# Down's seven-product pairs, GpSimd's transfers in up, and re-laid weights in an encoder block on one core

## The chip, the core and the metric

The kernel runs on one core of a Trainium2 chip. The metric is the device time of one execution in microseconds. Three runs of the kernel before gave 1123.14, 1123.25 and 1123.6 us, a median of 1123.25 us. The profile was taken on an execution of its own.

## The reference

One layer of an encoder: 256 tokens, model width 2048, feed-forward width 5632, all in float32. Every sub-layer is wrapped in RMS norms. `@` is a matrix product.

```python
hn = rmsnorm(h, mix_norm_pre)
z, xbc, dt_raw, u = split(hn @ w_in)
mix = concat(ssd_mixer(z, xbc, dt_raw), pool_mixer(u)) @ w_out
h = h + rmsnorm(mix, mix_norm_post)
hn = rmsnorm(h, ffn_norm_pre)
gate, val = split(hn @ w_up)                  # 2048 -> 2 x 5632
gate = dwconv_centred(gate, conv_w, conv_b)   # 3 taps along the tokens
ff = (gelu(gate) * val) @ w_down              # 5632 -> 2048
h = h + rmsnorm(ff, ffn_norm_post)
gate = sigmoid(rmsnorm(h, ple_norm_pre) @ w_ple_gate)
h = h + rmsnorm(gate * (p @ w_ple), ple_norm_post)
```

## The kernel before

**Products.** A float32 operand is kept as two parts, hi (rounded by ScalarE to the format that TensorE multiplies, L152) and lo (the rest, a subtraction on VectorE, L153). A product then takes three matmuls: hi by hi, hi by lo, lo by hi. `split` (L141) makes the two parts of a piece of weights; there are five buffers for hi parts and five for lo parts, and three for raw pieces as they come from memory (`raw`, L156). A raw piece is 128 partitions by 2048 values, 1 MB. All weights come through the DMA queue of one engine, SyncE (SP), in program order of the issues; a load waits there until its buffer is free.

**Stages in time.** dtu, xbc and z are the parts of the input projection, with the mixer's own work between their matmuls. wo is the output projection, ple0 the first half of the small projection of p. Then come up (11 groups `s`, each a gate block `ga` and a value block `va`), down (`dn`), ple1, the gate product (`gt`) and the tail. The stages stand behind one another on TensorE.

**Up.** `feature_pairs` (L340) computes 256 features: two raw pieces, each split in two halves of 1024 columns. There are 88 such raw pieces, here called slots. After each, `aside()` (L196) takes the next entry of the list `work` and runs its jobs: this is where work for later stages is laid aside. Behind the gate block stand the convolution (VectorE, L428), gelu (ScalarE, L884) and a multiplication by the row norm `rfb` on GpSimd (L885); behind the value block the product `hid` (VectorE, L895).

**Down.** `token_major` (L291) takes the hidden features in 22 pairs of 128, for each of two halves of the output columns. An ordinary pair (256 hidden features, 256 tokens, 1024 columns) takes 2 x 2 x 2 x 3 = 24 matmuls of 512 columns. A pair in `dn_fast` is a fast one: `seven_products` (L239) treats it as 2 x 2 blocks and needs seven block products in place of eight, 21 matmuls. For that it needs four sums of blocks on the hidden side (`hid_sums`, L920: four 128-wide VectorE operations, a ScalarE copy, a 512-wide VectorE operation) and four on the weights' side. `combine` (L269) adds the products up. Before, 12 of the 22 pairs of each half are fast; the hidden sums of four pairs (`dn_keep`) are kept in memory from the first half for the second.

**The weights' sums.** They are made during up. `block_sums` (L208) has a job `fetch` (load the piece of w_down into a page), two slots later `add` (`add_blocks`, L232: one 1024-wide and two 512-wide additions on VectorE), one slot later `store` (write the sums to DRAM). There are 28 blocks, 24 for down and 4 for the gate product, one every three slots; the last two are held in pages. In down a fast pair loads from DRAM the three raw blocks that it needs and the page of sums. All of these loads and stores go through SP's queue, among the weights, each behind the one before it (`load`, L116). There are 13 pages of 1 MB.

**Between down and gate.** `back` (L937), before pair 13 of the second half, loads h again, which was stored before up. `first_gate` (L943), before pair 16, loads the first piece of w_ple_gate and makes its parts apart from the splits: ScalarE writes the negated hi part, GpSimd issues a transfer that adds the weights to it, ScalarE writes hi. The dictionary `at` (L955) says where they stand.

**Order.** A scheduler puts the instructions of each engine in order when the kernel is built; every engine then works in that order. `tc.issue_after(x)` keeps an instruction behind x. Names in the profile: `ug_1l` is the lo part of a gate piece in up, `dnb` a block of w_down fetched for its sums, `dns` the stored sums, `hs` the parts of a hidden pair, `he`/`hd`/`hsum` its sums, `gtf` the first gate piece, `hb` h loaded again.

Of the kernel before, what the change touches and what calls it, by code (L numbers as in the profile page):

```python
# [11 lines left out]
F32 = mybir.dt.float32  # L12
# [4 lines left out]
P = 128  # L17
# [34 lines left out]
def build(nc, a, out):  # L52
    x = a["x"][0]
    w_in, w_out, w_up = a["w_in"][0], a["w_out"][0], a["w_ffn_up"][0]
    w_down, w_gate, w_ple = a["w_ffn_down"][0], a["w_ple_gate"][0], a["w_ple"][0]
    out = out[0]

    with tile.TileContext(nc) as tc, \
# [37 lines left out]
        c_dt = DSSD + 1536  # L96
        r0 = wp.tile([P, 2048], F32, tag="raw", bufs=3, name="dtur0")
        for n in range(2):
            first = ins(nc.scalar.dma_start(r0[:, n * 352:(n + 1) * 352],
                                            w_in[:P, c_dt + n * 352:c_dt + (n + 1) * 352]))  # L100
# [15 lines left out]
        def load(dst, src, ahead=False):  # L116

            with tc.issue_after(last["dma"]) if last and not ahead else nullcontext():
                return ins(nc.sync.dma_start(dst, src))

# [35 lines left out]
        def raw(name, src, a_, b_):  # L156
            r = wp.tile([P, 2048], F32, tag="raw", bufs=3, name=name)
            if src is None:
                return r
            last["dma"] = load(r[:, :a_ * b_].rearrange("p (a b) -> p a b", a=a_), src, True)  # L160
            return r
# [34 lines left out]
        def aside():  # L196

            for job in (work.pop(0) if work else ()):
                job()
# [32 lines left out]
        def add_blocks(r):  # L232

            v = r.rearrange("p (b c) -> p b c", b=4)
            nc.vector.tensor_add(v[:, 0:2], v[:, 0:2], v[:, 1::2])  # L235
            nc.vector.tensor_add(v[:, 3], v[:, 3], v[:, 0])
            nc.vector.tensor_add(v[:, 2], v[:, 2], v[:, 3])

        def seven_products(name, stage, w, k0, c0, a_, acc, alt, start, stop):  # L239
# [3 lines left out]
            if (stage, c0, k0) in sums_:  # L243
                r = raw(f"{name}r", None, 0, 0)
# [6 lines left out]
                b11 = split(f"{name}a", r[:, :512], 512)  # L251
                b2 = split(f"{name}b", r[:, 512:1536], 1024)
            else:
                r = t = raw(f"{name}r", w[k0 * P:(k0 + 2) * P, c0:c0 + 1024]
                            .rearrange("(k p) c -> p k c", p=P), 2, 1024)
                b11 = split(f"{name}a", r[:, :512], 512)
                b2 = split(f"{name}b", r[:, 1024:], 1024)
                add_blocks(r)
            t13 = split(f"{name}c", t[:, :1024], 1024)
            t42 = split(f"{name}d", t[:, 1024:], 1024)  # L260
            for x, (wh, wl), c, o, own in (
                    ("a11", b11, 0, alt[0], True), ("a12", b2, 0, acc[0][0], False), ("s4", b2, 512, acc[0][1], False),
                    ("s1", t13, 0, alt[1], True), ("s3", t13, 512, alt[2], True), ("a22", t42, 0, acc[1][0], False),
                    ("s2", t42, 512, alt[3], True)):
# [26 lines left out]
        def token_major(name, w, c0, ks, get, acc, tail=1, fast=(), alt=None, sums=None, at=()):  # L291
# [3 lines left out]
            for u in range(nu):  # L295
# [3 lines left out]
                if u in fast:  # L299
                    if u == fast[0]:  # L300
# [3 lines left out]
                r = None if f"{name}{k0}_0" in ready else raw(f"{name}r{k0}", w[k0 * P:(k0 + 2) * P, c0:c0 + 1024]  # L304
                                                               .rearrange("(k p) c -> p k c", p=P), 2, 1024)
# [8 lines left out]
                for t, (o, c), (k, wh, wl), q in order:  # L314
                    xh, xl = (v[:, t * P:(t + 1) * P] for v in get(k))
                    xx, ww = ((xh, wh), (xh, wl), (xl, wh))[q]
                    mm(o, xx, ww[:, c:c + o.shape[-1]], k == ks[0] and q == 0, k == ks[-1] and q == 2)
# [3 lines left out]
                aside()  # L321

        def feature_major(name, w, c0, get, acc):

            for u in range(4):
                r = raw(f"{name}r{u}", w[u * 512:(u + 1) * 512, c0:c0 + 512]
                        .rearrange("(k p) c -> p k c", p=P), 4, 512)
# [12 lines left out]
        def feature_pairs(name, w, c0, get, acc):  # L340


            for u in range(2):
                r = raw(f"{name}r{u}", w[u * 1024:(u + 1) * 1024, c0:c0 + 256]
                        .rearrange("(k p) c -> p k c", p=P), 8, 256)
# [8 lines left out]
                aside()  # L354
# [88 lines left out]
        for u in range(0, NK, 2):  # L443
            r = [wp.tile([P, 2048], F32, tag="raw", bufs=3, name=f"dtur{u}") if u else r0, page(f"dtur{u + 1}")]
            for j in range(2):
                k = u + j
                if k == 0:
                    last["dma"] = load(r[0][:, 704:1056], w_in[:P, c_dt + 704:c_dt + 1056])
# [3 lines left out]
                for c0, c1 in ((0, 704), (704, 1056)) if k == 1 else ((0, 1056),):  # L452
                    last["dma"] = load(r[j][:, c0:c1], w_in[k * P:(k + 1) * P, c_dt + c0:c_dt + c1])
# [29 lines left out]
        with tc.issue_after(half[0]), tc.issue_after(half[1]):  # L483
# [11 lines left out]
            for a_ in range(4):  # L495
# [17 lines left out]
        load(pmat.rearrange("p (g s t) -> p g s t", g=4, s=2),  # L513
             a["pool_matrix"].rearrange("g (s p) t -> p g s t", p=P))
        poolw = page("poolw")
        load(poolw.rearrange("p (g c d) -> p g c d", g=4, c=2),
             a["pool_w"][0].rearrange("g (c p) d -> p g c d", p=P))
# [122 lines left out]
        def xbc(slab):  # L640
            acc = main(f"xbc{slab}")
            feature_major(f"xb{slab}", w_in, DSSD + slab * 512, hn, acc)
# [29 lines left out]
        def skip(t):  # L672
            nc.gpsimd.tensor_tensor(by_head(y[:, t * 1024:(t + 1) * 1024]), by_head(xs[:, t * 1024:(t + 1) * 1024]),
                                    dsk.unsqueeze(2).to_broadcast([P, H, 64]), op=ALU.mult)

        def mix(t, g):
# [8 lines left out]
            nc.gpsimd.tensor_add(y[:, c0:c0 + 512], y[:, c0:c0 + 512], tm)  # L685
# [45 lines left out]
        token_major("z", w_in, 0, list(range(NK)), hn, zacc)  # L731
# [42 lines left out]
        def pair_sums(name, s, o, a11, a21, a12, a22):  # L774

            s1, s2, s3, s4 = (s[:, i * P:(i + 1) * P] for i in range(4))
# [5 lines left out]
            nc.vector.tensor_sub(o[:, 512:], s[:, :512], o[:, :512].bitcast(F32))  # L782
            return {f"s{i + 1}": (o[:, i * P:(i + 1) * P], o[:, 512 + i * P:512 + (i + 1) * P]) for i in range(4)}
# [81 lines left out]
        dn_fast, gt_fast, dn_keep = ((2, 3, 5, 7, 8, 10, 12, 13, 15, 16, 18, 19), (2, 3, 5, 7, 8, 10, 12, 13, 15, 16, 18, 19)), ((4, 6), (1, 2)), (3, 8, 13, 18)  # L865
# [4 lines left out]
        for i, w_ in enumerate(which[2:] + which[:2]):  # L870
            for j, jobs in enumerate(block_sums(*w_, i >= len(which) - 2)):
                work[3 * i + 2 + j].extend(jobs)
        hid = []
        for s in range(DFF // 512):
            sc = mid(f"gr{s}")
            for i in range(2):
                ga = main(f"ga{s}{i}")
                feature_pairs(f"ug{s}{i}", w_up, s * 512 + i * 256, hf, ga)
# [6 lines left out]
            nc.gpsimd.tensor_tensor(cv.rearrange("p (f t) -> p f t", f=4), cv.rearrange("p (f t) -> p f t", f=4),  # L885
                                    rfb.unsqueeze(1).to_broadcast([P, 4, L]), op=ALU.mult)
            for i in range(2):
                va = main(f"va{s}{i}")
                feature_pairs(f"uv{s}{i}", w_up, DFF + s * 512 + i * 256, hf, va)
# [9 lines left out]
        def get_hid(k):  # L899
            if k % 2 == 0:  # L900
                t = lp.tile([P, 1024], F32R, tag="hs", bufs=2, name=f"hs{k}")
                src = hid[k // 8][:, (k % 8) * L:(k % 8 + 2) * L]
                nc.scalar.copy(t[:, :512], src)  # L903
                nc.vector.tensor_sub(t[:, 512:], src, t[:, :512].bitcast(F32))  # L904
# [13 lines left out]
        keep, kept = [], {}  # L918

        def hid_sums(k):  # L920


            (h1, l1), (h2, l2) = get_hid(k), get_hid(k + 1)
            if k not in kept:
                src = hid[k // 8][:, (k % 8) * L:(k % 8 + 2) * L]
                n = dn_keep.index(k // 2) if k // 2 in dn_keep else -1
                if n >= 0 and n % 2 == 0:
                    keep.append(page(f"hsum{k}", F32R))
                o = keep[-1][:, n % 2 * 1024:(n % 2 + 1) * 1024] if n >= 0 else mid(f"he{k}", F32R)
                d = pair_sums(f"hd{k}", mid(f"hd{k}"), o, *(src[:, i * P:(i + 1) * P] for i in range(4)))  # L930
                if n >= 0:
                    kept[k] = d
            else:
                d = kept[k]
# [8 lines left out]
        def first_gate():  # L943

            r, hi, lo = page("gtf"), page("gtfh", F32R), page("gtfl", F32R)
            src = w_gate[:2 * P, :1024].rearrange("(k p) c -> p k c", p=P)
            last["dma"] = load(r.rearrange("p (k c) -> p k c", k=2), src)
            nc.scalar.activation(lo, r, AF.Copy, scale=-1.0)
            nc.gpsimd.dma_start(lo.rearrange("p (k c) -> p k c", k=2), src, accum_op=ALU.add)
            nc.scalar.copy(hi, r)  # L950
            for j in range(2):
# [3 lines left out]
                      fast=dn_fast, sums=hid_sums, at={13: back, 16: first_gate})  # L955
# [105 lines left out]
def constants():  # L1061
    return {"pool_matrix": pool_matrix()}
# [16 lines left out]
```

## Time and profile before

| | |
|---|---|
| median of three runs | 1123.25 us (1123.14 to 1123.6) |
| the profiled execution | 1123.11 us; its span 1121.3 us, 1.8 us around it |
| granted TensorE clock | 0.997 |
| transferred | 300.87 MB, mean 268 GB/s, 145996 packets, 98560 of them under 2 KB |
| GpSimd's own transfers | 272 packets, 1.05 MB (one transfer, `gtfl`) |

Stages on TensorE, by the chain of work in order of time: dtu to 52.6 us, xbc to 142.4, z to 198.7, wo to 287.1, ple0 and the start of up to 319.9, up to 789.0, down to 1016.7, ple1 and gate to about 1101, the tail to 1121.3.

How to read it: times are microseconds from the start of the span unless marked ns. PE is TensorE, PEld its weight loads, DVE VectorE, ACT ScalarE, POOL GpSimd, SP SyncE; "SPq" is an engine's queue of instructions that are not counted as busy. A row names the line of the kernel, the engine, the operation, output <- inputs, and how often. "[2.79 <-DMA x]" behind a row is idle time of that engine before the instruction, and what ended it. In a row of groups the number after the bar is the busy time, the next the mean of one in ns, and then the idle time before the group. "to landing" is from the issue of a transfer to its end. Busy times of pipelined neighbours overlap, so the pitch from start to start is a little under the duration shown.

### The profile page before, as it was taken

The numbers are of one execution on the slowest core, as the hardware profiler recorded it, in microseconds if no ns is written. First come the engines' busy times: TensorE is split into PE (matmuls) and PEld (weight loads), VectorE is DVE, ScalarE is ACT, GpSimd is POOL, SyncE is SP. The second block draws the span as 40 slices with busy tenths as digits, with TensorE's granted clock in tenths as the row PEclk, the third lists the DMA queues.
The fourth block names the chain that finished last, engine by engine and source line by source line (L and its number), as shares of the span: only waits on it lengthen the run. The fifth ranks groups of instructions, "written<-read, shape, count | busy, mean of one in ns | idle before, by whom it ended". The sixth has DMA issues, their size and how long they took to land.

```text
span 1121.3 us, 15775 instructions
## 1 busy us (share of the span) xinstructions
PE 1109.1 (99%) x5971; PEld 956.4 (85%) x5971; DVE 925.2 (83%) x1275; ACT 663.9 (59%) x927; POOL 76.2 (7%) x86
## 2 busy tenths in 40 slices
PE   9999999999999999999999999999999999999996
PEld 9999987888888888888888888888888888888875
DVE  6569895799898877877877768888899999889795
ACT  6847663555764554554545445445677777786672
POOL 0200004200110100000000000000000000001001
PEclk9999999999999999999999999999999999999998
DMA  9862447456789989989999898996969688995663
GB/s 363 310 207 96 170 161 269 151 188 190 252 308 347 328 300 336 314 289 309 333 330 314 276 330 289 325 304 224 339 185 334 221 286 301 383 318 177 230 235 109
DMA packets 145996, 300.87 MB, mean 268 GB/s; under 512 B 5504, under 2 KB 98560, under 8 KB 137856
## 3 DMA queue, kind: packets, MB, share of 16 engines
q1 hardware_dynamic: 145360, 298.45, 78.6%
q0 software_dynamic: 272, 1.05, 0.5%
q8 instruction: 47, 0.77, 0.3%
q10 hardware_dynamic: 288, 0.36, 0.1%
q14 instruction: 29, 0.24, 0.1%
HBM read 268.38 MB, written 31.46 MB: 267 GB/s over the span
## 4 chain that ended last, share of the span: by engine, by line
PE 96%; ACT 1%; DVE 1%; issue 1%; POOL 1%; POOLq 0%; DVEq 0%; ACTq 0%
PE va L87 22%; PE ga L87 21%; PE dna L87 14%; PE woa L87 7%; PE xbc L87 6%; PE gt L87 5%; PE dtu L87 4%; PE z L87 4%; PE dns L87 3%; PE dn0s L87 1%; PE dn1s L87 1%; PE ple L87 1%; PE pw L87 1%; PE yd L87 0%; PE gts L87 0%
## 5 line engine op out<-in xcount | busy, mean ns | idle before, releaser
L87 PE MATMUL ga<-wox,ug_0h 128*128 128x512 f32 x352 | 125.5, 395 | 0.0
L87 PE MATMUL ga<-wox,ug_1h 128*128 128x512 f32 x352 | 125.1, 394 | 0.0
L87 PE MATMUL va<-wox,uv_1h 128*128 128x512 f32 x352 | 124.8, 393 | 0.0
L87 PE MATMUL va<-wox,uv_0h 128*128 128x512 f32 x352 | 124.8, 393 | 0.0
L87 PE MATMUL ga<-wox,ug_1l 128*128 128x256 f32 x352 | 99.1, 282 | 0.0
L87 PE MATMUL ga<-wox,ug_0l 128*128 128x256 f32 x352 | 99.1, 282 | 0.0
L87 PE MATMUL va<-wox,uv_1l 128*128 128x256 f32 x352 | 99.1, 281 | 0.0
L87 PE MATMUL va<-wox,uv_0l 128*128 128x256 f32 x352 | 99.1, 281 | 0.0
L87 PEld LDWEIGHTS va<-wox,uv_1h 128*128 128x128 f32 x352 | 66.1, 188 | 15.0
L87 PEld LDWEIGHTS va<-wox,uv_0h 128*128 128x128 f32 x352 | 66.1, 188 | 15.0
L87 PEld LDWEIGHTS ga<-wox,ug_0h 128*128 128x128 f32 x352 | 66.1, 188 | 14.9
L87 PEld LDWEIGHTS ga<-wox,ug_1h 128*128 128x128 f32 x352 | 66.1, 188 | 14.9
L87 PEld LDWEIGHTS ga<-wox,ug_0l 128*128 128x128 f32 x352 | 66.2, 188 | 0.1
L87 PEld LDWEIGHTS ga<-wox,ug_1l 128*128 128x128 f32 x352 | 66.2, 188 | 0.0
L87 PEld LDWEIGHTS va<-wox,uv_0l 128*128 128x128 f32 x352 | 66.2, 188 | 0.0
L87 PEld LDWEIGHTS va<-wox,uv_1l 128*128 128x128 f32 x352 | 66.2, 188 | 0.0
L885 POOL TENSOR_TENSOR fc<-fc,rfb 128x1024 f32<-128x1024 f32 x11 | 28.0, 2547 | 438.6 <-ACT fc L884 438.6
L87 PE MATMUL dna<-dn_0h,hs 128*128 128x512 f32 x160 | 50.1, 393 | 0.0
L87 PE MATMUL dna<-dn_1h,hs 128*128 128x512 f32 x160 | 49.9, 393 | 0.0
L235 DVE TENSOR_TENSOR dnb<-dnb 128x1024 f32<-128x1024 f32 x24 | 30.8, 1283 | 17.8 <-DMA dnb<-w_ffn_down 17.6
L903 ACT CAST hs<-hid 128x512 fp32r<-128x512 f32 x44 | 27.2, 617 | 23.2 <-PE dna L87 14.8
L904 DVE TENSOR_TENSOR hs<-hid,hs 128x512 fp32r<-128x512 f32 x44 | 30.2, 686 | 9.8 <-ACT hs L903 9.7
(1903 smaller groups left out, 3105.3 us busy)
## 6 DMA issues: line engine op xcount, KB each, us to landing
dnb<-w_ffn_down SPq DMA_DIRECT2D x24, 1024.0 KB, 10.4
dns<-dnb SPq DMA_DIRECT2D x22, 1024.0 KB, 7.4
dn0r<-w_ffn_down SPq DMA_DIRECT2D x10, 1024.0 KB, 6.0
dn1r<-w_ffn_down SPq DMA_DIRECT2D x10, 1024.0 KB, 7.1
zr<-w_in SPq DMA_DIRECT2D x8, 1024.0 KB, 5.1
dtur<-w_in SPq DMA_DIRECT2D x14, 528.0 KB, 8.7
wo0r<-w_out SPq DMA_DIRECT2D x7, 1024.0 KB, 5.6
wo1r<-w_out SPq DMA_DIRECT2D x6, 1024.0 KB, 5.5
```

Of the source, the lines that this page charges most:

```text
L87: last["pe"] = ins(nc.tensor.matmul(o, lhsT, rhs, start=start, stop=stop, skip_group_check=True))
L235: nc.vector.tensor_add(v[:, 0:2], v[:, 0:2], v[:, 1::2])
L885: nc.gpsimd.tensor_tensor(cv.rearrange("p (f t) -> p f t", f=4), cv.rearrange("p (f t) -> p f t", f=4), rfb.unsqueeze(1).to_broadcast([P, ...
L903: nc.scalar.copy(t[:, :512], src)
L904: nc.vector.tensor_sub(t[:, 512:], src, t[:, :512].bitcast(F32))
```

## The change

1. All weights are laid out anew on the host, in contiguous pieces of 128 x 2048 values as the kernel loads them, so that each partition's row is 8 KB (up had 1 KB rows, down 4 KB). In the pieces for pairs the blocks stand as B12, B11, B21, B22, so a fast pair loads its three raw blocks with one transfer of 6 KB rows.
2. Fast pairs in down: 14 of 22 per half, before 12. The hidden sums of eight pairs (`dn_stored`) are made during up by jobs of their own, stored to DRAM and loaded again in both halves of down; `dn_keep` is gone. The order of the seven products changes.
3. 32 block sums (28 for down, 4 for gate), fetched at slot 5*i//2 + 5, added three slots later, stored one slot after that. The addition is four 512-wide operations, each on the result of the one before.
4. The fetches, the stores, and the stores and loads of the hidden sums are issued by GpSimd (`load_aside`), in program order. Ahead of each slot's jobs GpSimd copies one column of the lo part of that slot's second half (`pace`), so the jobs' transfers go out when VectorE has written that part.
5. The multiplication by `rfb` in up, `skip` and the addition of `ym` in z move from GpSimd to VectorE.
6. `back` and the first gate piece (`first`) move from pairs 13 and 16 of down's second half to behind its last pair.

```diff
+        def load_aside(dst, src):
+
+            with tc.issue_after(last["aside"]) if "aside" in last else nullcontext():
+                last["aside"] = ins(nc.gpsimd.dma_start(dst, src))
...
-        def aside():
-
-            for job in (work.pop(0) if work else ()):
+        def aside(lo=None):
+
+            jobs = work.pop(0) if work else ()
+            if jobs and lo is not None:
+
+                with tc.issue_after(last["aside"]) if "aside" in last else nullcontext():
+                    last["aside"] = ins(nc.gpsimd.tensor_copy(tiny("pace", 1), lo[:, :1].bitcast(F32)))
+            for job in jobs:
                 job()
...
-                load(r.rearrange("p (k c) -> p k c", k=2),
-                     w[k * P:(k + 2) * P, c0:c0 + 1024].rearrange("(k p) c -> p k c", p=P))
+                load_aside(r, w[c0 // 1024, k // 2])
...
-                    load(t, pg[0])
+                    load_aside(t, pg[0])
...
-            return [fetch], [], [add], [store]
+            return [fetch], [], [], [add], [store]
...
-            nc.vector.tensor_add(v[:, 0:2], v[:, 0:2], v[:, 1::2])
-            nc.vector.tensor_add(v[:, 3], v[:, 3], v[:, 0])
-            nc.vector.tensor_add(v[:, 2], v[:, 2], v[:, 3])
+            for i, j in ((1, 0), (0, 3), (3, 1), (2, 3)):
+                nc.vector.tensor_add(v[:, i], v[:, i], v[:, j])
...
-                last["dma"] = load(r[:, 512:1536], w[(k0 + 1) * P:(k0 + 2) * P, c0:c0 + 1024], True)
-                last["dma"] = load(r[:, :512], w[k0 * P:(k0 + 1) * P, c0:c0 + 512], True)
+                last["dma"] = load(r[:, 512:], w[c0 // 1024, k0 // 2][:, 512:], True)
...
-                aside()
+                aside(wl)
...
-            nc.gpsimd.tensor_add(y[:, c0:c0 + 512], y[:, c0:c0 + 512], tm)
+            nc.vector.tensor_add(y[:, c0:c0 + 512], y[:, c0:c0 + 512], tm)
...
-        dn_fast, gt_fast, dn_keep = ((2, 3, 5, 7, 8, 10, 12, 13, 15, 16, 18, 19), (2, 3, 5, 7, 8, 10, 12, 13, 15, 16, 18, 19)), ((4, 6), (1, 2)), (3, 8, 13, 18)
+        dn_fast, gt_fast = ((2, 3, 4, 5, 7, 8, 9, 11, 12, 13, 15, 16, 18, 19), (2, 3, 4, 5, 7, 8, 9, 11, 12, 13, 15, 16, 18, 19)), ((4, 6), (1, 2))
+
+        dn_stored = (2, 3, 5, 8, 11, 13, 16, 19)
...
-                work[3 * i + 2 + j].extend(jobs)
-        hid = []
+                work[5 * i // 2 + 5 + j].extend(jobs)
+        hid, kept = [], {}
...
+        def hid_sums_jobs(k):
+
+            o = []
+
+            def make():
+                o.append(lp.tile([P, 1024], F32R, tag="hs", bufs=2, name=f"he{k}"))
+                hid_sums_of(k, o[0][:, 512:].bitcast(F32), o[0])
+
+            def store():
+                kept[k] = dp.tile([P, 1024], F32, tag=f"hsum{k}", bufs=1, name=f"hsum{k}")
+                load_aside(kept[k], o[0].bitcast(F32))
+
+            return [make], [store]
+
+        for u in dn_stored:
+            for j, jobs in enumerate(hid_sums_jobs(2 * u)):
+                work[u // 2 * 8 + u % 2 * 2 + 6 + j].extend(jobs)
...
-            nc.gpsimd.tensor_tensor(cv.rearrange("p (f t) -> p f t", f=4), cv.rearrange("p (f t) -> p f t", f=4),
+            nc.vector.tensor_tensor(cv.rearrange("p (f t) -> p f t", f=4), cv.rearrange("p (f t) -> p f t", f=4),
...
+            o = mid(f"hd{k}", F32R)
+            if k in kept:
+                load_aside(o.bitcast(F32), kept[k])
+                d = sums_in(o)
             else:
-                d = kept[k]
+                d = hid_sums_of(k, sp.tile([P, 512], F32, tag="junk", bufs=1, name=f"hs{k}"), o)
...
-                      fast=dn_fast, sums=hid_sums, at={13: back, 16: first_gate})
+                      fast=dn_fast, sums=hid_sums, at={NF // 2: lambda: (back(), first())})
...
+    def tiles(w, nk, nc):
+
+        k, c = w.shape
+        return w.reshape(k // P // nk, nk, P, c // nc, nc).transpose(3, 0, 2, 1, 4).reshape(c // nc, k // P // nk, P, nk * nc)
+
+    def pairs(w):
+
+        r = tiles(w, 2, 1024)
+        return np.concatenate([r[..., 512:1024], r[..., :512], r[..., 1024:]], axis=-1)
```

More of the change, by code (lines that the diff above doesn't have):

```diff
@@ L53, in build @@
     x = a["x"][0]
-    w_in, w_out, w_up = a["w_in"][0], a["w_out"][0], a["w_ffn_up"][0]
-    w_down, w_gate, w_ple = a["w_ffn_down"][0], a["w_ple_gate"][0], a["w_ple"][0]
+    w_dtu, w_xbc, w_z, w_out, w_up = a["w_dtu"], a["w_xbc"], a["w_z"], a["w_out_"], a["w_up"]
+    w_down, w_gate, w_ple = a["w_down"], a["w_gate"], a["w_ple_"]
     out = out[0]
@@ L1033, in cols @@
         return np.concatenate([v.reshape(-1, P).T for v in vs], axis=1)
-    return {
+    def tiles(w, nk, nc):
[4 more added lines that the diff above has]
+        return np.concatenate([r[..., 512:1024], r[..., :512], r[..., 1024:]], axis=-1)
+    w_in, c_dt = a["w_in"][0], DSSD + 1536
+    return {
+        "w_z": pairs(w_in[:, :DSSD]),
+        "w_xbc": tiles(w_in[:, DSSD:c_dt], 4, 512),
+        "w_dtu": tiles(w_in[:, c_dt:], 1, 1056)[0],
+        "w_out_": pairs(a["w_out"][0]),
+        "w_up": tiles(a["w_ffn_up"][0], 8, 256).reshape(2, DFF // 512, 2, 2, P, 2048),
+        "w_down": pairs(a["w_ffn_down"][0]),
+        "w_gate": pairs(a["w_ple_gate"][0]),
+        "w_ple_": pairs(a["w_ple"][0]),
+        "pool_w_": a["pool_w"][0].reshape(8, P, 256).transpose(1, 0, 2).reshape(P, 2048),
         "x_cols": np.concatenate([cols(a["mix_norm_pre"][0]),
@@ L1068 @@
     arrays.update({n: np.ascontiguousarray(v) for n, v in laid_out(arrays).items()})
-    arrays.update(constants())
+    arrays.update({n: np.ascontiguousarray(v) for n, v in constants().items()})
     for n in ("p", "mix_norm_pre", "ssd_conv_w", "ssd_conv_b", "ssd_norm", "pool_scale", "ffn_norm_pre",
-              "ffn_conv_w", "ple_norm_pre", "ffn_conv_b", "ssd_dt_bias", "ssd_a_log", "ssd_d"):
+              "ffn_conv_w", "ple_norm_pre", "ffn_conv_b", "ssd_dt_bias", "ssd_a_log", "ssd_d", "w_in", "w_out",
+              "w_ffn_up", "w_ffn_down", "w_ple_gate", "w_ple", "pool_w"):
         del arrays[n]
```

97 lines of the change are left out of this document (42 added, 55 removed).

## Prediction

> **What bounds the kernel now.** I began with the page's head and its chain of work.
>
> ```profile
> span 1121.3 us, 15775 instructions
> PE 1109.1 (99%) x5971; PEld 956.4 (85%) x5971; DVE 925.2 (83%) x1275; ACT 663.9 (59%) x927; POOL 76.2 (7%) x86
> PE 96%; ACT 1%; DVE 1%; issue 1%; POOL 1%; POOLq 0%; DVEq 0%; ACTq 0%
> ```
>
> TensorE is busy 99% of the span, and 96% of the chain is its own matmuls. Work taken from TensorE shortens the run; another engine matters only once it makes TensorE wait. The chain in order of time (start, duration, what) gives the price of a matmul:
>
> ```profile
> 766.63 22.33 PE va L87 x128
> 788.96 11.11 PE dna L87 x48
> ...
> 809.75 5.55 PE dna L87 x24
> ...
> 1016.74 3.45 PE ple L87 x15
> ```
>
> In down, 24 matmuls take 5.55 us, 0.2313 us each. Each half has 10 ordinary pairs of 24 matmuls and 12 fast pairs of 21: 2 x (240 + 252) = 984, times 0.2313 = 227.6 us. Down lasts from 788.96 to 1016.74, 227.8 us. It has no stall to win back; only fewer matmuls help.
>
> Busy time by stretch (length; then PE, PEld, DVE, ACT, POOL, granted clock, DMA share, GB/s), two halves of up and two of down:
>
> ```profile
> 319.90:554.40 234.50, 234.50 (x1346) 205.85 (x1345) 191.66 (x239) 119.70 (x158) 15.66 (x6) 1.00 0.95 317
> 554.40:789.00 234.60, 234.60 (x1346) 205.93 (x1345) 186.40 (x241) 115.60 (x155) 12.35 (x5) 1.00 0.91 297
> 789.00:905.00 116.00, 116.00 (x504) 94.27 (x503) 107.44 (x149) 83.70 (x112) 0.00 (x0) 1.00 0.77 262
> 905.00:1016.70 111.70, 111.65 (x484) 90.34 (x483) 102.56 (x140) 82.51 (x104) 3.78 (x8) 1.00 0.91 324
> ```
>
> The clock is full, so nothing is to be had there. Second come VectorE (0.81 of up, 0.92 of down) and the DMA engines (0.91 to 0.95 in up). These two carry what the change adds.
>
> **The change part by part.**
>
> *Two more fast pairs per half.* 4 pairs x 3 matmuls = 12 fewer, all on the chain: 12 x 0.2313 = **-2.78 us**.
>
> *VectorE in down.* The starts of equal neighbours give the pitch of an operation:
>
> ```profile
> 1010.39 0.69 DVE L282 TENSOR_TENSOR dna<-dna,dn1v 128x512 f32<-128x512 f32 x1
> 1010.99 0.68 DVE L283 TENSOR_TENSOR dn1v<-dn1s,dn1v 128x512 f32<-128x512 f32 x1
> ...
> 1012.79 1.21 DVE L153 TENSOR_TENSOR ple_0l<-ple1r,ple_0h 128x1024 fp32r<-128x1024 f32 x1
> 1013.92 1.22 DVE L153 TENSOR_TENSOR ple_1l<-ple1r,ple_1h 128x1024 fp32r<-128x1024 f32 x1
> ```
>
> 512 wide costs 0.60 us, 1024 wide 1.13. A fast pair with stored hidden sums has three wide splits, one narrow and one hidden split: 3 x 1.13 + 2 x 0.60 = 4.59 us, under its 21 x 0.2313 = 4.86 on TensorE. One that still computes its sums adds four 128-wide operations (an estimate of 0.2 each, their 0.29 us row below less the same overlap) and a 512-wide one: 5.99. An ordinary pair needs 2.86 against 5.55. A half then holds 8 x 4.59 + 6 x 5.99 + 8 x 2.86 = 95.5 us beside 486 x 0.2313 = 112.4 of TensorE; before, 12 x 5.99 + 10 x 2.86 = 100.5, less where sums were kept. The longest run without an ordinary pair, 7 to 9, costs 1.1 - 0.3 + 1.1 = 2 us of lead, no more than two computed neighbours before. So 0; without the stored sums it would be 8 x 1.4 = 11 us of VectorE per half.
>
> *DMA in down.* A half loads 8 pieces of 1.05 MB, 14 of 0.79, 14 block sums of 1.05 (two less in the first half, held) and 8 hidden sums of 0.52: 38.3 MB, 36.2 in the first, 342 and 323 GB/s over 112 us. The row of the second half moved 324 GB/s at a share of 0.91, 356 at a full one, with rows of 4 and 2 KB; now they have 8 and 6. I take 0; bounds 0 and +6 us (38.3 MB at 324 GB/s last 118 us).
>
> *Mixing in z.* y + ym goes from GpSimd to VectorE:
>
> ```profile
> 186.45 2.18 POOL L685 TENSOR_TENSOR y<-y,ym 128x512 f32<-128x512 f32 x1 [6.00 <-DVE ym L683]
> 188.66 0.69 DVE L690 TENSOR_TENSOR y<-y,yd 128x512 f32<-128x512 f32 x1 [1.16 <-POOL y L685]
> ...
> 189.41 2.00 PE L87 MATMUL yd<-xs,E 128*128 128x64 f32 x16 [0.19 <-DVE y L690]
> ```
>
> 2.18 us become 0.69 and TensorE's wait (0.19 us and a matmul group that began late) goes: **-0.4 us**, bounds -1 and 0. skip, also moved, falls in xbc beside TensorE's own work: 0.
>
> *VectorE in up.* What it gains and loses, as groups (line, engine, operation, count | busy us, mean ns | idle before, releaser):
>
> ```profile
> L235 DVE TENSOR_TENSOR dnb<-dnb 128x1024 f32<-128x1024 f32 x23 | 29.6, 1286 | 17.8 <-DMA dnb<-w_ffn_down 17.6
> L237 DVE TENSOR_TENSOR dnb<-dnb 128x512 f32<-128x512 f32 x24 | 18.6, 774 | 0.3
> ...
> L236 DVE TENSOR_TENSOR dnb<-dnb 128x512 f32<-128x512 f32 x24 | 16.4, 685 | 0.2
> ```
> ```profile
> L780 DVE TENSOR_TENSOR hd<-hid,hd 128x128 f32<-128x128 f32 x17 | 4.9, 290 | 0.4
> ```
> ```profile
> 462.08 2.41 POOL L885 TENSOR_TENSOR fc<-fc,rfb 128x1024 f32<-128x1024 f32 x1 [42.56 <-ACT fc L884]
> 463.33 2.24 DVE L153 TENSOR_TENSOR uv_1l<-uv31r,uv_1h 128x1024 fp32r<-128x1024 f32 x1 [1.41 <-ACT uv_1h L152]
> ```
>
> The fc multiply adds 11 x 1.22 = 13.4 us. The block sums cost 32 x 4 x 0.69 = 88.3 instead of 28 x (1.29 + 0.77 + 0.69) = 77.0: +11.3. Eight hidden sums cost 8 x (4 x 0.29 + 0.69) = 14.8. Against this, a split that meets GpSimd's multiply takes 2.24 us instead of 1.22, so up to 11 x 1.0 are saved; I take 10. VectorE goes from 191.7 + 186.4 = 378.1 to 407.6 us of up's 469.1, and has 61 us idle, **1.9 us for each of the 32 fetched blocks**. Busy time alone hides. The question is what VectorE waits for.
>
> *The fetch on GpSimd.* Before, SP's queue fetched each block early. Now the fetch goes out when VectorE has written the lo part of a unit, GpSimd has read one column of it (81 such pace copies), and GpSimd has issued the transfer. In the changed kernel's order of instructions, the block's first add stands on VectorE on average 5.3 us of work behind that lo part (mostly two splits; 2.3 to 10.8). VectorE works in order: if the block is not there, the splits behind the add wait, and after them TensorE. That can be carried for a while:
>
> ```profile
> 480.07 1.22 DVE L153 TENSOR_TENSOR ug_1l<-ug41r,ug_1h 128x1024 fp32r<-128x1024 f32 x1 [0.46 <-ACT ug_1h L152]
> 484.08 1.22 DVE L235 TENSOR_TENSOR dnb<-dnb 128x1024 f32<-128x1024 f32 x1 [2.79 <-DMA dnb<-w_ffn_down]
> ```
>
> VectorE stood 2.79 us for a block, and TensorE lost nothing: five lo buffers of 22.33 / 8 = 2.79 us each (a piece of the chain uses eight) let VectorE be up to some 10 us ahead. So with L the time from lo part to landed block, nothing is lost while L is under 5.3 + 1.9 + 10 / 32 = **7.5 us**; above it, each 0.1 us costs 3.2 us over the 32 blocks. For L:
>
> ```profile
> h_kept<-h SPq DMA_DIRECT2D x2, 1024.0 KB, 4.5
> ```
> ```profile
> dnb<-w_ffn_down SPq DMA_DIRECT2D x24, 1024.0 KB, 10.4
> ```
> ```profile
> 980.63 1.43 POOL L949 DMA_DIRECT2D gtfl<-w_ple_gate x1 [203.62 <-ACT gtfl L948]
> ```
> ```profile
> DMA to landing us min/median/max: 14.4/14.4/14.4
> ```
>
> A 1 MB transfer with 8 KB rows on a quiet queue lands 4.5 us after its issue by SP. GpSimd's issue is longer by at most 1.43, say 1.1; the pace copy and its wake-up add 0.5 (estimate from GpSimd's small operations). That is 6.1 us. The same lo part frees a weight buffer, so 1 MB of weights starts with the fetch; both share the engines, about half of 1 MB at 423 GB/s (the busiest 3 us, quoted below) = 1.2. L = **7.3 us**. The far end is 14.4 + 0.5 = 14.9 (gtfl, an adding transfer in a full stretch); the near one 6.1. I take 7.3, since h_kept is the row nearest in shape and queue. That is under 7.5, so 0, but by little.
>
> ```profile
> 997.00:1000.00 3.00, 3.00 (x15) 2.46 (x14) 2.74 (x4) 2.70 (x3) 0.00 (x0) 1.00 1.04 423
> ```
>
> The Trainium skill bears on this price. "DMA: Bandwidth & Descriptors", section "Bandwidth", gives 6.15 us of engine time for 1 MB issued from GpSimd, without making the descriptors. By that, L would be 0.5 + 1.4 + 6.15 = 8.1 and the loss 19 us, an estimate from that page; no run here yet shows a plain transfer from GpSimd.
>
> *Down to gate.* h and the first gate piece now come behind down's last weights.
>
> ```profile
> 991.31 2.72 SPq L119 DMA_DIRECT2D dn1r<-w_ffn_down  x2
> ```
> ```profile
> 1022.92 0.63 PE L87 MATMUL gt<-gtfh,dnxh 128*128 128x512 f32 x2
> 1023.38 0.63 PE L87 MATMUL gt<-gtfl,dnxh 128*128 128x512 f32 x2
> ```
>
> SP issued down's last weights by 994.0, after the change about 991. With 10.4 us to land, the gate piece is there at 1002; ScalarE's negated copy (some 2 us behind its queue) and GpSimd's issue bring 1006; 14.4 more, as measured, make 1020.4. TensorE asks for it at 1023.4 - 2.8 = 1020.6. Nothing in hand. ScalarE's copies now stand near the end of down. I take **+0.3 us**, bounds 0 and +4.
>
> Sum against the profiled execution (1123.11 us, 0.14 under the median): 1123.11 - 2.78 - 0.4 + 0.3 = 1120.2; against the median 1120.4. I forecast **1120.3 us**, with 1119.2 to 1121.0 as this case's own range.
>
> **The rivals.**
>
> 1. *The paced fetch starves VectorE* (slower). The row at 463.33 shows how: a split that began while GpSimd read memory took 1.02 us longer and ended 1.0 us after GpSimd did. If a split starts right behind the lo part, the pace copy has to wait for its end, about 0.9 us, and L is 8.2: 32 x 0.7 = 22 us, **1142 us**. It decides from L = 7.5. For it: when VectorE is late, its next split always follows at once, so lateness feeds itself. Against it: a VectorE that is ahead waits for TensorE's buffers, so the copy finds it idle. The Trainium skill, "SBUF — State Buffer", states this as an exclusive lock that a VectorE operation with two inputs in SBUF and a GpSimd operation that reads SBUF hold against each other; the row agrees.
> 2. *The gate piece is late* (about no change). With L of gtfl 2 to 4 us longer, TensorE waits as long: 1122 to 1124, **1122.5 us**. For: the margin of 0.2 us. Against: behind down's weights the queue is less full than at 980.
> 3. *Down becomes bound by transfers*: +6 as above, **1126 us**. Against it: longer rows.
> 4. *The change does not do what it says*: the matmuls in the order are 12 fewer, so this would need down's fast pairs to wait for GpSimd's hidden sums, 16 loads; priced as rival 3.
>
> **How the numbers follow.** Forecast 0.45, rival 1 0.34, rival 2 0.11, rivals 3 and 4 0.10. About 0.2% (2.25 us) can be told from no change here, so faster is under 1121.0, slower over 1125.5. Faster: the forecast, 0.45. Same: rival 2 and a mild form of 1 and 3 (0.02), 0.13. Slower: the rest, 0.42. The range: rival 1 spreads with L from 1126 (7.7 us) to 1174 (9.2); a third of it, 0.11, lies over 1148 (8.4). With 0.03 under 1119.2 and a little of the others, 1119.2 to 1148 leaves out less than 0.2.
>
> **What would show it.** In the changed profile: 972 matmuls in down at 0.231 us; VectorE's idle time before the blocks' first adds (17.6 us before) under 60 us and up's pieces still 22.33 us; fetches landing within about 7 us of the pace copy. Pieces of 23 us or more, and waits of TensorE for lo parts in up, would show rival 1. A wait of gt for gtfl shows rival 2; waits for dn pieces or hidden sums in down, rivals 3 and 4. What would make me wrong above all is the 4.5 us taken for a transfer that GpSimd issues.

## The result, and the profile after

The changed kernel takes 1208.66 us (median of 5 runs, 1206.04 to 1211.68) against 1123.25: a ratio of 1.076, interval [1.074, 1.078]. It is slower by 85 us. The profiled execution took 1211.68 us, its span 1209.9.

The head of its page and its chain:

```profile
span 1209.9 us, 16043 instructions
PE 1134.8 (94%) x5959; PEld 972.9 (80%) x5959; DVE 938.3 (78%) x1347; ACT 664.8 (55%) x935; POOL 107.0 (9%) x236
PE 54%; DMA 19%; DVE 13%; issue 8%; ACT 3%; POOL 2%; DVEq 0%; POOLq 0%; ACTq 0%
DMA dnb<-w_down 16%; PE dna L88 12%; PE woa L88 6%; PE xbc L88 5%; PE gt L88 5%; PE dtu L88 4%; PE z L88 4%; PE dns L88 3%; PE ga L88 3%; PE va L88 3%; DMA gtb<-w_gate 3%; DVE dnb L243 2%; DVE ug_1l L157 2%; DVE ug_0l L157 2%; PE dn0s L88 2%
```

The instructions on TensorE are 12 fewer, as the change says. But the chain, 96% TensorE before, is now 54% TensorE; 19% of it is the fetching of blocks (`dnb`, `gtb`). The groups say who waited. On VectorE the block additions (count 112 = 28 x 4) had 145.7 us of idle time ahead of them, 144.5 of it for the fetch; before, it was 17.8. TensorE waited for lo parts behind those additions:

```profile
L243 DVE TENSOR_TENSOR dnb<-dnb 128x512 f32<-128x512 f32 x112 | 77.1, 688 | 145.7 <-DMA dnb<-w_down 144.5
...
L88 PE MATMUL ga<-wox,ug_0l 128*128 128x256 f32 x352 | 104.9, 298 | 34.6 <-DVE ug_0l L157 34.6
...
L88 PE MATMUL va<-wox,uv_0l 128*128 128x256 f32 x352 | 103.9, 295 | 22.4 <-DVE uv_0l L157 22.3
...
L88 PE MATMUL va<-wox,uv_1l 128*128 128x256 f32 x352 | 100.1, 284 | 2.7 <-DVE uv_1l L157 2.7
```

By stretch, up and down (columns as before):

```profile
400.00:554.40 154.40, 133.20 (x716) 114.50 (x717) 106.75 (x156) 61.21 (x84) 18.78 (x44) 0.96 0.75 283
554.40:700.00 145.60, 128.73 (x699) 111.14 (x698) 102.36 (x150) 57.25 (x81) 18.82 (x45) 0.94 0.79 294
...
875.20:990.00 114.80, 114.80 (x500) 93.32 (x499) 105.03 (x134) 86.45 (x112) 4.30 (x8) 1.00 0.83 317
990.00:1096.00 106.00, 106.00 (x461) 86.24 (x460) 98.79 (x129) 81.22 (x96) 4.59 (x9) 1.00 0.96 376
```

In up, nobody is full: in the first row TensorE 0.86, VectorE 0.69, the DMA engines 0.75. That is how a chain of waits looks. In down TensorE is full, without a stall.

Where the 88.6 us of span went, from the chain's pieces:

```profile
875.21 11.11 PE dna L88 x48
...
1171.98 16.75 PE gt L88 x73
```
```profile
1084.78 16.75 PE gt L87 x73
```

The second fence is the kernel before. Down begins at 875.21 instead of 788.96: +86.2 us by the end of up. From there to the last gate block it is 296.8 us instead of 295.8: +1.0, though 12 matmuls (2.8 us) are gone, so 3.7 us were lost behind down. From that block to the end it is 37.9 instead of 36.5: +1.4. Sum: 88.6.

The 86.2 us have two parts. Over the whole of up (from 319.9 us to its end) TensorE stands for 59.7 us, which is just what it waits for lo parts there (34.6 + 22.4, and 2.7 for `uv_1l`). The rest is no waiting: the same 2690 matmuls are busy for 495.7 us instead of 469.1, at a mean granted clock of 0.95 instead of 1.00. So some 27 us of the loss are slower matmuls that come with the stalls.

**One fetch in detail**, in the stretch from 658 to 673 us: VectorE, GpSimd and SyncE.

```profile
658.97 1.22 DVE L157 TENSOR_TENSOR uv_1l<-uv61r,uv_1h 128x1024 fp32r<-128x1024 f32 x1
...
662.63 1.22 DVE L157 TENSOR_TENSOR ug_1l<-ug70r,ug_1h 128x1024 fp32r<-128x1024 f32 x1
671.13 2.15 DVE L243 TENSOR_TENSOR dnb<-dnb 128x512 f32<-128x512 f32 x3 [7.28 <-DMA dnb<-w_down]
```
```profile
655.18 0.53 POOL L123 DMA_DIRECT2D dns<-dnb  x1
660.32 0.18 POOL L205 COPY pace<-uv_1l 128x1 f32<-128x1 f32 x1 [4.61 <-DVE uv_1l L157]
660.87 0.54 POOL L123 DMA_DIRECT2D dnb<-w_down  x1 [0.36 <-issue]
663.98 0.19 POOL L205 COPY pace<-ug_1l 128x1 f32<-128x1 f32 x1 [2.58 <-DVE ug_1l L157]
664.43 0.53 POOL L123 DMA_DIRECT2D dns<-dnb  x1 [0.26 <-issue]
```
```profile
660.22 3.99 SPq L118 DMA_DIRECT2D ug71r<-w_up  x2
```
```profile
661.00:662.00 1.00, 1.00 (x8) 0.87 (x7) 0.98 (x2) 0.62 (x1) 0.41 (x1) 1.00 0.99 410
...
666.00:667.00 1.00, 1.00 (x7) 0.87 (x6) 0.00 (x0) 0.00 (x0) 0.00 (x0) 1.00 0.97 401
...
670.00:671.00 1.00, 0.00 (x0) 0.00 (x0) 0.00 (x0) 0.00 (x0) 0.00 (x0) 1.00 0.93 369
```

The lo part ends at 660.19. The pace copy starts 0.13 us later and takes 0.18 us; the issue starts at 660.87, 0.7 us behind the lo part. So pacing and issuing cost little. VectorE reaches the block's first addition at 663.85 and stands until 671.13. The last fence shows why: the DMA engines are full, at about 400 GB/s. In the fetch's 10.2 us they moved about 4 MB: the block, two weight pieces issued between 660.2 and 664.2, and parts of two stores of older sums. TensorE has run dry by 670. The medians are like this one:

```profile
dnb<-w_down POOLq DMA_DIRECT2D x28, 1024.0 KB, 10.1
dns<-dnb POOLq DMA_DIRECT2D x26, 1024.0 KB, 9.8
```

So L, from lo part to landed block, is 0.7 + 10.1 = 10.8 us. The 28 fetches for down differ among themselves: while the eight that landed in 6.7 to 7.3 us were under way, the engines moved 2.2 to 2.5 MB in all; while the fifteen that took 10 us or more were, 3.7 to 5.4 MB (each worked out from the GB/s of its own stretch). That fits engines that are shared; no run took the other traffic away to test it.

### The profile page after: what moved, and what is told of

It is laid out like the page before. It is cut to its first block, busy times and chain, and to the rows that moved or that the text cites. A ratio compares the mean times of both kernels' runs of the same rounds, so it can differ in the third digit from the quotient of the medians.

```text
span 1209.9 us, 16043 instructions
## 1 busy us (share of the span) xinstructions
PE 1134.8 (94%) x5959; PEld 972.9 (80%) x5959; DVE 938.3 (78%) x1347; ACT 664.8 (55%) x935; POOL 107.0 (9%) x236
## 4 chain that ended last, share of the span: by engine, by line
PE 54%; DMA 19%; DVE 13%; issue 8%; ACT 3%; POOL 2%; DVEq 0%; POOLq 0%; ACTq 0%
DMA dnb<-w_down 16%; PE dna L88 12%; PE woa L88 6%; PE xbc L88 5%; PE gt L88 5%; PE dtu L88 4%; PE z L88 4%; PE dns L88 3%; PE ga L88 3%; PE va L88 3%; DMA gtb<-w_gate 3%; DVE dnb L243 2%; DVE ug_1l L157 2%; DVE ug_0l L157 2%; PE dn0s L88 2%
## 5 line engine op out<-in xcount | busy, mean ns | idle before, releaser
L243 DVE TENSOR_TENSOR dnb<-dnb 128x512 f32<-128x512 f32 x112 | 77.1, 688 | 145.7 <-DMA dnb<-w_down 144.5
L88 PE MATMUL ga<-wox,ug_0l 128*128 128x256 f32 x352 | 104.9, 298 | 34.6 <-DVE ug_0l L157 34.6
L88 PE MATMUL ga<-wox,ug_0h 128*128 128x512 f32 x352 | 134.3, 415 | 0.0
L88 PE MATMUL va<-wox,uv_0h 128*128 128x512 f32 x352 | 132.5, 411 | 0.0
L88 PE MATMUL va<-wox,uv_0l 128*128 128x256 f32 x352 | 103.9, 295 | 22.4 <-DVE uv_0l L157 22.3
L426 ACT ACTIVATE fc<-gr,vt 128x256 f32<-128x256 f32 x44 | 24.1, 594 | 152.6 <-DVE gr L914 152.6
L88 PEld LDWEIGHTS ga<-wox,ug_0l 128*128 128x128 f32 x352 | 71.0, 202 | 37.8 <-DVE ug_0l L157 37.8
L88 PE MATMUL dna<-dn_1h,hs 128*128 128x512 f32 x128 | 40.6, 393 | 0.0
L88 PE MATMUL dna<-dn_0h,hs 128*128 128x512 f32 x128 | 40.3, 393 | 0.0
L784 ACT CAST he<-he 128x512 fp32r<-128x512 f32 x8 | 5.0, 620 | 59.3 <-DVE he L783 59.3
## 6 DMA issues: line engine op xcount, KB each, us to landing
dnb<-w_down POOLq DMA_DIRECT2D x28, 1024.0 KB, 10.1
```

The source lines that it names most:

```text
L88: last["pe"] = ins(nc.tensor.matmul(o, lhsT, rhs, start=start, stop=stop, skip_group_check=True))
L243: nc.vector.tensor_add(v[:, i], v[:, i], v[:, j])
L426: nc.scalar.activation(o, i, AF.Identity, bias=vec(bcol + f), scale=vec(wcol + half * wstep + f))
L784: nc.scalar.copy(o[:, :512], s[:, :512])
```

## The experiments

Theory 1: the first addition stands too close behind its fetch in VectorE's fixed order, and the fetch is late because it shares the DMA engines. Rival A: VectorE has too much work in up, or is blocked by GpSimd's copies. Rival B: a transfer is slow because GpSimd issues it. The scheduler orders all instructions anew for each kernel, so an edit can also move work that it does not name.

**1. Later additions.** One line: each block's first addition is kept behind the lo parts of its own slot.

```diff
             def add():
-                add_blocks(pg[0])
+                with tc.issue_after(last["dve"]):
+                    add_blocks(pg[0])
```

> The changed kernel, with one line more: each block's first addition may stand on VectorE only behind the lo parts of its own slot. In the order of instructions the work between the pacing lo part and the first addition grows from 5.3 us (two splits) to 13.8 us (six splits) on average; nothing else changes. Theory 1 (the addition stands too close behind its fetch; the fetch lands some 10.5 us behind the lo part, because it shares the transfer engines with weights and stores): VectorE's waits before the additions fall from 159 us to under 25 us, up's pieces are 22.33 us again, and the time is about 1211.7 - 86 = 1125 us, 1122 to 1128 (the 5 us lost behind down stay). Rival A (VectorE has too much work in up, or is held up by GpSimd's copies): waits for the blocks go, but up stays long; over 1145 us. Rival B (GpSimd's transfers take longer the more are under way, so a larger window is used up as well): over 1145 us, with the transfers' time to landing over 14 us.

Measured: 1123.59 us, ratio 1.0003 [0.9994, 1.0011]: the 85 us are gone. Up by stretch, VectorE's block additions, and the fetches:

```profile
319.90:554.40 234.50, 234.50 (x1346) 205.81 (x1345) 199.00 (x286) 120.05 (x160) 45.32 (x80) 1.00 0.91 340
554.40:789.00 234.60, 234.60 (x1346) 205.90 (x1345) 196.39 (x279) 117.71 (x158) 42.79 (x74) 1.00 0.91 341
```
```profile
L244 DVE TENSOR_TENSOR dnb<-dnb 128x512 f32<-128x512 f32 x112 | 76.8, 685 | 0.8
```
```profile
dnb<-w_down POOLq DMA_DIRECT2D x28, 1024.0 KB, 10.8
```

TensorE is full again. The fetch takes as long as before (10.8 us to landing), and VectorE's wait is 0.8 us instead of 145.7. Same issuer, same copies, same work: rival A falls, and the place of the addition is shown to be the cause. The program asks for the addition three slots behind the fetch; the scheduler had put it some two splits behind the lo part that lets the fetch go (5.3 us of work), and the new line makes that six (13.8 us).

**2. No pace copies** in the changed kernel, the additions where the scheduler puts them.

```diff
-                aside(wl)
+                aside()
```

> The changed kernel without the pace copies: GpSimd issues fetches and stores as soon as their pages allow, still in program order. The additions stand close behind each other in the order of instructions as the scheduler sees fit. Theory 1: the distance between fetch and addition decides, not who issues; fetches go out earlier, so most of the 86 us go away: 1125 to 1160 us (transfers that are not paced may delay weights). Rival B (a transfer issued by GpSimd is slow in itself): it stays over 1190 us.

Measured: 1143.74 us, ratio 1.018 [1.017, 1.020]. Three quarters of the loss go, though a fetch now takes 13.0 us to landing (median). VectorE still waits:

```profile
DVE dnb L243 <- DMA dnb<-w_down: 75.1, 20, 8.9
```

**3. Fetches and stores on SyncE**, no pace copies.

```diff
-                load_aside(r, w[c0 // 1024, k // 2])
+                load(r, w[c0 // 1024, k // 2])
...
-                    load_aside(t, pg[0])
+                    load(t, pg[0])
```

> The changed kernel without the pace copies and with the block fetches and stores on SyncE's queue among the weights, as before the change (GpSimd keeps the hidden sums' transfers). Everything else of the change stays: 14 fast pairs, 32 blocks in four additions, fc's multiplication on VectorE, the new layout. Theory 1: up runs at 22.33 us a piece as before, 1122 to 1127 us. Rival A (VectorE's additional 30 us of work in up are what stops it): over 1140 us.

Measured: 1122.72 us, ratio 0.9994 [0.9985, 1.0003]. Up is about as long as before, with 18 us more of VectorE's busy time in it (396.5 us against 378.1): again against rival A. VectorE hardly waits for blocks:

```profile
DVE dnb L243 <- DMA dnb<-w_down: 0.5, 1, 0.5
```

**4. h and the gate piece at their old places**, with late additions (`at={13: back, 16: first}`).

> The first experiment's kernel (late additions) with h and the first gate piece loaded at pairs 13 and 16 of down's second half, as before the change. The changed kernel lost 3.7 us between down's end and the last gate block against before: ScalarE stood for the gate piece (1.3 us) and for a later weight piece of the gate (1.8 us) in its order. If that comes from the late loads, this kernel is 2.5 to 4 us faster than the first experiment's, and if theory 1 holds too, about 1120 to 1122 us. Rival: the loss comes from ScalarE's order of squares and splits alone; then under 1 us of difference. Rival: loading them amid down's weights costs as much there.

Measured: 1125.45 us, ratio 1.002 [1.001, 1.003]; 1.9 us slower than experiment 1. The expectation falls. TensorE's wait for dnxh goes, but in down's second half TensorE now stands 1.7 us, where experiment 6 and the changed kernel have none:

```profile
905.00:1018.00 113.00, 111.31 (x474) 88.23 (x474) 102.27 (x133) 85.61 (x108) 9.84 (x14) 1.00 0.92 359
```

The gate piece's 3.8 us of copies on ScalarE and h's 2 MB stand in that stretch; which of the two does it was not tried.

**5. Who issues.** On top of experiment 1, one of two h loads and one of two h stores are issued by GpSimd.

> The first experiment's kernel (late additions), with one of the two h loads before the output projection and one of the two h_kept stores behind it issued by GpSimd, the other one by SyncE as before: pairs of transfers of 1 MB with 8 KB rows, at the same time. Theory 1 (the fetch was late because it shares the engines, not because of who issued it): from issue to landing the GpSimd ones take at most 1.5 us more than their SyncE partners, so about 5 to 6.5 us for the store (4.5 us median of both by SyncE before). Rival B (slow in itself): over 9 us for the store in that quiet stretch.

Measured, issue to landing (one execution, 1123.15 us):

```profile
h<-x POOLq DMA_DIRECT2D x1, 1024.0 KB, 10.3
h<-x SPq DMA_DIRECT2D x1, 1024.0 KB, 6.8
h_kept<-h POOLq DMA_DIRECT2D x1, 1024.0 KB, 4.3
h_kept<-h SPq DMA_DIRECT2D x1, 1024.0 KB, 6.1
```

The loads are no pair: GpSimd's went out 20 us earlier than SyncE's, among weights. The stores were issued 1 us apart in a quiet stretch: GpSimd's landed in 4.3 us, SyncE's, behind it, in 6.1. In this one pair, a transfer is not slow because GpSimd issues it. Against rival B.

**6. The gate piece ahead of h**, both behind down, with late additions.

```diff
-                      fast=dn_fast, sums=hid_sums, at={NF // 2: lambda: (back(), first())})
+                      fast=dn_fast, sums=hid_sums, at={NF // 2: lambda: (first(), back())})
```

> The first experiment's kernel with the first gate piece loaded ahead of h, both behind down's last pair. There the gate piece landed late, so ScalarE stood 1.8 us for it, GpSimd's adding transfer ran beside a later gate piece, that piece took 6.9 us, and ScalarE stood 1.4 us for it with dnxh queued behind. Theory (2.1 us are lost behind down because h's 2 MB stand ahead of the gate piece): 1.2 to 2 us faster than the first experiment, 1121.6 to 1122.4 us. Rival (the later gate piece waits for its buffer, not for the traffic): within 0.5 us of the first experiment's 1123.6, or slower if h is late instead.

Measured: 1121.61 us, ratio 0.9986 [0.9977, 0.9995]: 2 us faster than experiment 1. There ScalarE's order had stood for a later gate piece with dnxh behind it:

```profile
1018.97 0.83 ACT L193 ACTIVATE dnxh<-dnxt,vt 128x256 fp32r<-128x256 f32 x2
1021.23 1.04 ACT L156 CAST gt_0h<-gt0r 128x1024 fp32r<-128x1024 f32 x1 [1.43 <-DMA gt0r<-w_gate]
1022.18 0.83 ACT L193 ACTIVATE dnxh<-dnxt,vt 128x256 fp32r<-128x256 f32 x2
```

Here four pairs of dnxh operations stand ahead of the cast that waits, not one, and TensorE no longer waits for dnxh. The time is the expected one, the reason is not: the piece that this cast waits for takes 8.5 us to landing, against 6.9 in experiment 1. So the gain came with ScalarE's order, which the swap also altered, and less traffic is not shown to be the cause.

**7. SyncE's queue with late additions and the swap.**

> The kernel with fetches and stores on SyncE's queue and no pace copies, with late additions and the gate piece ahead of h. That kernel before it had a tail 1.4 us shorter than all the kernels in which GpSimd issues the fetches, lost 0.5 us in up to late blocks, and 1.5 us behind down. If late additions take away the first and the swap half of the second loss: 1120.0 to 1121.5 us, faster than the kernel before by 0.2%. Rival: the changes only move the waits, 1122 to 1123.5 us.

Measured: 1133.79 us, ratio 1.009 [1.008, 1.011]. The expectation falls. SyncE's queue, among whose weights the stores stand, waited for additions that now come later (us in all, times, longest); in experiment 3 that wait was 17.3 us:

```profile
SPq L118 <- DVE dnb L244: 101.8, 15, 9.7
```

and the weights behind the stores came late (in up ScalarE now waited 6.7 us for `ug90r` and 5.5 for `ug60r`). Late additions go with a queue of their own.

**8. Paced, but issued by SyncE.** GpSimd's copy writes into the page, and SyncE's load waits for it.

```diff
-                load_aside(r, w[c0 // 1024, k // 2])
+                with tc.issue_after(last["aside"]) if "aside" in last else nullcontext():
+                    last["aside"] = ins(nc.gpsimd.tensor_copy(r[:, :1], last["lo"][:, :1].bitcast(F32)))
+                load(r, w[c0 // 1024, k // 2], True)
```

> The changed kernel, with the fetches issued by SyncE but still paced: GpSimd's copy of the lo column writes into the page first, and SyncE's load of the block has to wait for it. In this build's order of instructions 6.9 us of VectorE's work stand between lo part and first addition (5.3 us in the changed kernel). Theory 1: pacing and sharing make the fetch late, not GpSimd; it lands some 9 us behind the lo part, and up still loses 15 to 60 us: 1140 to 1185 us. Rival B (GpSimd's issue is what is slow): the fetch lands within 6 us, and the time is 1122 to 1130 us.

Measured: 1158.23 us, ratio 1.031 [1.029, 1.033].

```profile
DVE dnb L246 <- DMA dnb<-w_down: 87.3, 23, 8.6
```
```profile
dnb<-w_down SPq DMA_DIRECT2D x28, 1024.0 KB, 9.0
```

Issued by SyncE, a paced fetch takes 9.0 us, and VectorE waits for it in the same way. Rival B falls.

**9. Twelve pairs** per half in experiment 6's kernel.

> The best kernel so far (late additions, the gate piece ahead of h, 1121.6 us) with 12 fast pairs per half again, those of the kernel before, and 7 stored hidden sums; all else as there. If the 12 matmuls taken from down are the gain, they cost 12 x 0.2313 = 2.8 us: 1124.1 to 1124.7 us. Rival (other waits in down take part of it up): under 1.5 us of difference, 1121.6 to 1123.1.

Measured: 1125.07 us, ratio 1.0014 [1.0005, 1.0023], 3.5 us above experiment 6 and a little above the expected range. Down's last matmul starts at 1015.25 us instead of 1012.38, 2.9 us later: the 12 matmuls are worth about their 2.8 us. The last gate block is another 1.4 us late, 1.1 of it a wait that this kernel has behind down, and the end of the span is 0.9 us shorter. With the fast pairs, four block sums and one hidden sum went too; their share is not separated.

```profile
PE dnxt L385 <- DVE dnxl L194: 1.1, 1, 1.1
```

**10. Experiment 6 without pace copies.**

> The best kernel so far (1121.6 us) without the pace copies: fetches go out as soon as their pages allow, additions still behind the lo parts of their own slot. If the place of the addition is all that counts, the time stays: 1121 to 1122.5 us. Rival (pacing is needed so that transfers do not delay weights): 1124 us or more, with waits of TensorE for lo parts in up.

Measured: 1121.22 us, ratio 0.9979 [0.9970, 0.9988], the fastest version, though 0.4 us from experiment 6 is too little to tell the two apart. With the additions late, pacing has nothing left to do here.

**11. Hidden sums reloaded by SyncE**, on top of experiment 10.

```diff
-                load_aside(o.bitcast(F32), kept[k])
+                last["dma"] = load(o.bitcast(F32), kept[k], True)
```

> The best kernel so far (late additions, gate piece ahead of h, no pace copies, 1121.2 us) with the 16 reloads of hidden sums in down on SyncE's queue. Between VectorE's last operation and the end of the span lie 3.8 us with 1 or 25 transfers issued by GpSimd in the kernel, 4.2 with 57, 5.2 with 85. If that time goes with the count of GpSimd's transfers, 69 of them give 4.4 to 5.0 us, and the kernel gains 0.2 to 0.8 us: 1120.4 to 1121.0. Rival: it goes with something else in up, and the end stays at 5.2; and the reloads, each waiting in SyncE's order for a buffer that a product must free, hold up down's weights: 1121.5 us or more.

Measured: 1125.93 us, ratio 1.0025 [1.0015, 1.0034]. The end of the span got shorter, from 5.2 to 4.1 us behind VectorE's last operation, but the last gate block came 5.3 us later: the reloads hold up down's weights, since SyncE waits in order for products to free their buffers. (The traces have 55, 87 and 71 transfers issued by GpSimd where the expectation says 57, 85 and 69.)

```profile
SPq L118 <- PE dn1s L88: 40.6, 6, 9.2
```

## Why the prediction was wrong

The forecast, 1120.3 us, was far off, and the range, to 1148, did not reach 1208.7. The effect, a paced fetch that starves VectorE, was named as rival 1, but with the smaller chance, a price of 22 us and another cause.

- **The step that failed** is the price of the fetch, "both share the engines, about half of 1 MB at 423 GB/s ... = 1.2", so L = 7.3. In a quiet stretch a store of that size takes 4.3 us (experiment 5; I had taken 4.5, and named just this figure as the likeliest fault), and pace copy and issue 0.7 (I had 1.6). But the fetch shares the engines with two weight pieces and two stores, not with half of one piece: 10.1 us to landing, 5.8 us over the quiet figure where I had 1.2. That the 5.8 us come from sharing is argued from the full engines, not tested by itself. I counted only what the same lo part releases. The row of the kernel before for the very same fetch, 10.4 us, was quoted and not used.
- **Rival 1's own mechanism** was not it either. It had the pace copy wait 0.9 us for VectorE's next operation. GpSimd's copies by themselves (ns: least, median, most):

```profile
L205 POOL COPY pace<-uv_1l x41: 177/307/583, 320.3 to 865.1; 128x1 f32<-128x1 f32 x41
L205 POOL COPY pace<-ug_1l x40: 183/186/2787, 338.7 to 848.2; 128x1 f32<-128x1 f32 x40
```

  One took 2.8 us; both medians are under a third of a microsecond. And experiment 1 has all 81 of them, one of 4.0 us, and loses nothing in up.
- **The threshold is only a rough rule.** "Nothing is lost while L is under 7.5; above it, each 0.1 us costs 3.2 us" gives 32 x 3.3 = 106 us for the measured L, against 86 measured. In experiment 8 (6.9 us of work, so a threshold of 9.1; L = 0.8 + 9.0, with 0.8 from lo part to issue in the fetch at 573 us) it gives 22 against the 34.6 that it lies above experiment 1. So it is too high once and too low once, and it knows nothing of the slower clock, 27 of the 86 us. Of its parts, the 5.3 us between lo part and addition fits: 10.8 - 5.3 = 5.5 us of waiting per block, where VectorE's waits for fetches are 144.5 + 14.2 us, 5.0 for each of 32. The idle time per block was 2.3 us rather than 1.9 (73.7 us in experiment 1's up).
- **VectorE's work in up**: forecast 407.6 us, measured 395.4 over the same stretch in experiment 1. The total was 3% off and on the safe side, but the added work was 17 us, not 29.5.
- **12 matmuls, -2.8 us**: right (down without a stall; experiment 9, as far as it separates them). **Down's transfers, 0**: right, at 376 GB/s in its second half. **z, -0.4**: z took 55.8 us instead of 56.2. Right.
- **Down to gate, +0.3**: it was +3.7. TensorE did not wait for gtfl, as rival 2 had it. It waited 2.1 us for dnxh, which ScalarE's order had put behind a later piece that ScalarE waited 1.8 us for. gtf, too, kept ScalarE 1.3 us, but right behind its copies ScalarE stood 2.6 us for down, so that wait is not shown to have cost time. Experiment 1, in the same order, loses 2.1 us there at a granted clock of 1.00. In the changed kernel the clock is 0.91 from 1096 to 1115 us, so the other 1.6 us are likely the clock's, which is not tested.
- **The end**: +1.4 us that the prediction did not have.

With late additions, the gate piece ahead of h and no pace copies (experiment 10) the change is worth about 2 us.

## What to carry to other kernels

Price a transfer under load by all that the engines move until it lands, over their full rate (here 4 MB at about 400 GB/s for a block of 1 MB); its time in a quiet stretch is only the lower end. Where a trace has the same transfer under the same load, that row is the estimate, whoever issues it. In an engine that works in order, look at how much work stands between the start of a load and its first use, and lengthen that before anything else: here one line that moved the use back was worth 85 us.

## What was not expected of the hardware

**The end of the span is longer where GpSimd issues many transfers.** VectorE's last rows, of the kernel before and of experiment 1:

```profile
1114.79 2.74 DVE L987 SCALAR_TENSOR_TENSOR vg<-vg,go1r,hb 128x512 f32<-128x512 f32 x4 [0.80 <-POOL go1r L982]
```
```profile
1113.73 2.74 DVE L1010 SCALAR_TENSOR_TENSOR vg<-vg,go1r,hb 128x512 f32<-128x512 f32 x4 [0.81 <-POOL go1r L1005]
```

The spans end at 1121.3 and 1121.7, so 3.8 and 5.2 us later, though the same last stores follow. Over the kernels, with the number of transfers that GpSimd issued: 1: 3.8; 25: 3.8 and 3.9; 55: 4.2; 71: 4.1; 76: 4.3; 87: 5.2 (six kernels, the changed one among them); 89: 5.4. The difference lies behind the last stores: the DMA engines are empty from 1119.8 us in the kernel before and from 1118.7 in experiment 1, and 1.5 and 3.0 us pass with nothing busy. What is done in that time no row shows; whether the count is the cause stays open.

**TensorE's granted clock** fell to 0.94 to 0.96 in the stretches of up with stalls, and was 1.00 in those shown without. Over up it was 0.95, and 469.1 / 0.95 = 494 us is close to the 495.7 that the matmuls took. Yet in experiment 2, where TensorE stands 18.1 us in up, it is 1.00 there. Which stalls lower it stays open.
